# Order of X's updates, early squares, and two ordinary pairs ahead, in a Hymba-style encoder layer

## Chip, cores and metric

The kernel runs on one core of a Trainium2 chip (trn2). The metric is the device time of one execution in microseconds, the median of several runs. Beside the runs there is one profiled execution, whose span (first to last instruction) and trace are used for reading.

## Reference

One encoder layer over 256 tokens with a width of 2048, everything in fp32:

```python
for layer in range(DEPTH):          # DEPTH = 1
    ff = swiglu(rms_norm(x, pre_norm_ffn1), w_ffn1_gate_up, w_ffn1_down)     # D_FF = 5632
    x = x + 0.5 * rms_norm(ff, post_norm_ffn1)
    h = rms_norm(x, pre_norm_mix)
    q_h, i_h, f_fwd, f_bwd, g_h, q_a, k_a, v_a = split(h @ w_mix_in)
    y_h = hgrn2_mixer(...)          # gated linear recurrence, both directions, chunks of 64
    y_a = window_attention(...)     # 8 heads, 2 kv heads, +-128 tokens, sink and T5 bias
    x = x + rms_norm(concat(y_h, y_a) @ w_mix_out, post_norm_mix)
    ff = swiglu(rms_norm(x, pre_norm_ffn2), w_ffn2_gate_up, w_ffn2_down)
    x = x + 0.5 * rms_norm(ff, post_norm_ffn2)
return x
```

with `swiglu(x, wg, wd) = (silu(gate) * up) @ wd`. Nearly all of the work is in five large matrix products: two gate/up projections, two down projections and the mixer's two projections.

## The kernel before

**Products.** A fp32 product is made of three passes: each operand is split into a high part h (rounded to fp32r, a cast on ScalarE, L176) and the rest l (a subtraction on VectorE, L177), and TensorE adds h·h, h·l and l·h (`three`, L423; L352 to L354 for the mixer's first products, L299 and L304 elsewhere). The activations lie transposed in X^T as h and l parts (`xt` for X, `ht` for the FFN's inner values). Weights come in blocks of 1 MB: SP issues a DMA into `raw` (three buffers), ScalarE and VectorE split it into `h` and `l` (five buffers each).

**Pairs.** A down projection runs over 22 pairs, each two blocks of 128 of the 5632 inner columns, twice: run 0 for the first 1024 output columns, run 1 for the others. An ordinary pair costs 24 matmuls of 512 columns. A *seven* pair (the even ones below 20) saves three with a scheme of seven products in place of eight; for it VectorE makes in-place sums of the raw block (L455, L459, L461) and ScalarE and VectorE split those, and its first left operand with its right block is the separate `ha`, `la`. While a seven is split, the code already loads the ordinary pair that follows it and splits its first half (`begin_next`, `AHEAD`). The order of pairs is a list, `orders[0]` for run 0 and `orders[1]` for run 1, used by both FFNs. Pair 1 is worked first, then the transposes of the last gate/up group (silu at L884, L885, transposes at L896) and then `first_run` does the rest.

**End of a projection.** `Pairs.finish` ends run 1. It holds back the last two pairs and multiplies them block by block: m is a half of the 256 rows, n a half of the run's columns, q = 0..3 a quarter of X's 2048 columns. For each block it makes the row's sum of squares (`squares`, L612, ScalarE), multiplies by the gain (`gains`, L619, VectorE), and after both n it adds the normed result to X (`update(m, q)`, L666, VectorE). X's quarters are then transposed on TensorE (`turned(m, q)`, L210), and the new X^T is taken as h by ScalarE (`hi`, L227) and as l by VectorE (`lo`, L232). So that TensorE has work in between, the first products of the next projection are laid among these steps (`lead`, a `LeadN` for the mixer and a `Gated` for FFN2; `lead.more(i)` splits half of its second block, `lead.pieces(m, xt)` gives groups of products). This happens twice, behind FFN1 (707 to 741 us, "end 1") and behind the mixer (1125 to 1160 us, "end 2"). The end of FFN2 has code of its own.

In these blocks the order on TensorE, VectorE and ScalarE is the one written (`manual_schedule`), and instructions that come from outside of the block are filled in by the scheduler. Everywhere else the scheduler puts the instructions in order by its own costs. SP's loads go in the order of the program.

**Statistics of the next norm.** `pre_stats` (L240) makes the squares of X, eight of 512 columns on ScalarE (L249), then VectorE's sum, GpSimd's power and a copy into `rs2`. `spread` (L262) makes a diagonal matrix of them (`dg`, L267, VectorE), multiplies it by ones on TensorE (L268) to get the scales along the free axis, and copies these to `R`; X^T is multiplied by them later (`even`). It is done at the start, behind end 1 and behind end 2.

**Start.** X is loaded in pieces, transposed and taken while the first gate/up products run, in a block written by hand (L958 to L1020).

Of the kernel before, what the change touches and what calls it, by code (L numbers as in the profile page):

```python
# [11 lines left out]
F32 = mybir.dt.float32  # L12
# [3 lines left out]
BF16 = mybir.dt.bfloat16  # L16
AF = mybir.ActivationFunctionType
# [3 lines left out]
P = 128  # L21
D = 2048
# [3 lines left out]
EPS = 1e-6  # L26
# [11 lines left out]
def hymba_layer_kernel(  # L38
# [25 lines left out]
    nc = tc.nc  # L64
# [11 lines left out]
    def nm(s):  # L76
        uid[0] += 1
        return f"{s}_{uid[0]}"
# [11 lines left out]
    res = {"X": new_X()}  # L90
# [89 lines left out]
    def rsqrt_of(ssq, scale, eps):  # L180
        tot = stat.tile([P, 1], F32, tag="tot", name=nm("tot"))
        nc.vector.tensor_reduce(tot, ssq, axis=AX.X, op=ALU.add)
        v = stat.tile([P, 1], F32, tag="v", name=nm("v"))
        nc.vector.tensor_scalar(v, tot, scale, eps, ALU.mult, ALU.add)
        r = stat.tile([P, 1], F32, tag="r", name=nm("r"))
        nc.gpsimd.tensor_tensor(r, v, mhalf[:, 0:1], ALU.pow)
        return r
# [41 lines left out]
    def take_lo(*a):  # L229

        for src, g, hi, lo in take_views(*a):
            nc.vector.scalar_tensor_tensor(  # L232
                lo, src, g, hi.bitcast(F32), ALU.mult, ALU.subtract
            )
# [5 lines left out]
    def pre_stats():  # L240
        with tc.issue_after(last["act"].ins):
            pre_stats_now()

    def pre_stats_now():
        for m in range(2):
            ssq = stat.tile([P, 4], F32, tag="ssq", name=nm("ssq"))
            for q in range(4):
                jk = stat.tile([P, 512], BF16, tag="jk", name=nm("jk"), bufs=1)
                nc.scalar.activation(  # L249
                    jk, res["X"][:, m, q * 512 : (q + 1) * 512], AF.Square, accum_out=ssq[:, q : q + 1]  # L250
                )
            r = rsqrt_of(ssq, 1.0 / D, EPS)
            last["rs2"] = nc.vector.tensor_copy(rs2[:, m : m + 1], r)

    def power_and_rest():
# [284 lines left out]
    class Pairs(Blocks):  # L540
# [75 lines left out]
        def gains(self, m, n, dst=None):  # L616
            if dst is None:
                dst = self.y[m, 2 * self.now + n]
            nc.vector.tensor_tensor(  # L619
                dst, self.c[m][n], self.pg[:, n * 512 : (n + 1) * 512], ALU.mult  # L620
            )
# [9 lines left out]
        def finish(self, mul, post, new_x=None, gain=None, lead=None):  # L631


            order = self.orders[1]
            n_order = len(order)
            self.post = post
            self.work(n_order - self.HELD)
            held = []
            for u in order[n_order - self.HELD :]:
                held.append((u, *split_load(self.source(u), hp=post, lp=post)))  # L640
            close_far()
            self.half_gain(post)
            if new_x:
                new_x()
            X = res["X"]
            if lead:
                lead.load()
            r = [None, None]
            y = self.y

            def products(m, n, part):
                for u, k, hs, ls in [
                    (u, k, hs, ls) for u, hs, ls in held for k in range(2)
                ][part]:
                    self.plain(u, hs, ls, m, n, k)

            def squares(m, n):
                self.squares(m, n)
                if n == 1:
                    r[m] = rsqrt_of(self.ssq[m], 1.0 / (D * mul * mul), EPS / (mul * mul))  # L660

            gains = self.gains

            def update(m, q):
                sl = slice(q * 512, (q + 1) * 512)
                nc.vector.scalar_tensor_tensor(  # L666
                    X[:, m, sl], y[m, q], r[m], X[:, m, sl], ALU.mult, ALU.add
                )

            def update_aside(m, q):  # L670
                sl = slice(q * 512, (q + 1) * 512)
                nc.scalar.mul(y[m, q], y[m, q], r[m])
                nc.gpsimd.tensor_tensor(X[:, m, sl], X[:, m, sl], y[m, q], ALU.add)

            ordered = {mybir.EngineType.PE, mybir.EngineType.DVE, mybir.EngineType.Activation}
            every = slice(None)
            if gain is None:
                def store(m, q):
                    sl = slice(q * 512, (q + 1) * 512)
                    nc.sync.dma_start(out[0, m * P : (m + 1) * P, sl], X[:, m, sl])  # L680

                def in_place(n):
                    gains(1, n, dst=self.c[1][n])
                    y[1, 2 + n] = self.c[1][n]

                with tc.manual_schedule(engines=ordered):
                    products(0, 0, every)
                    squares(0, 0)
                    gains(0, 0)
                    products(0, 1, every)  # L690
                    squares(0, 1)
                    gains(0, 1)
# [24 lines left out]
            def hi(m, q):  # L717
                take_hi(m, q, gain, xt, banks[m, q])

            def lo(m, q):  # L720
                take_lo(m, q, gain, xt, banks[m, q])

            with tc.manual_schedule(engines=ordered):
                products(0, 0, every)
                squares(0, 0)
                gains(0, 0)
                products(0, 1, every)
                squares(0, 1)
                update(0, 0)
                gains(0, 1)  # L730
                products(1, 0, every)
                lead.more(0)
                update(0, 1)
                squares(1, 0)
                gains(1, 0)
                products(1, 1, slice(0, 3))

                def took(m, q):
                    hi(m, q)
                    lo(m, q)  # L740

                turned(0, 0)
                took(0, 0)
                products(1, 1, slice(3, None))
                turned(0, 1)
                squares(1, 1)
                took(0, 1)
                update(1, 0)
                update(1, 1)
                lead.more(1)  # L750
                first, second = lead.pieces(0, xt), lead.pieces(1, xt)
                next(first)
                next(first)
                turned(1, 0)
                took(1, 0)
                gains(1, 1)
                next(first)
                turned(1, 1)
                took(1, 1)
                for _ in first:  # L760
                    pass
                for m, q in ((0, 2), (1, 2), (0, 3), (1, 3)):
                    update(m, q)
                    next(second)
                    turned(m, q)
                    took(m, q)
                for _ in second:
                    pass
            return xt

# [66 lines left out]
    def ffn(gated, w_dn, post_gain, again, gain=None, lead=None, aside=None):  # L837

        with ExitStack() as st:
# [74 lines left out]
            for g in range(NG):  # L914
# [39 lines left out]
    xt = new_xt()  # L954
    gated.see(xt)
    with tc.manual_schedule():
        banks = {}

        def turned(*at):
            banks[at] = turn(*at)  # L960
# [48 lines left out]
        gated.piece(0, 1, 0)  # L1009
        gated.piece(0, 1, 1)  # L1010
        gated.parts[1] = split(raws[0])
        turned(0, 1)
        turned(1, 1)
        taken(0, 1)
        taken(1, 1)
        for k in range(2):
            for m in range(2):
                gated.piece(1, k, m)
        gated.parts[2] = split(raws[1])
        for k in range(2):  # L1020
            for m in range(2):
                gated.piece(2, k, m)
                turned(m, 2 + k)
# [503 lines left out]
```

## Time and profile before

| | |
|---|---|
| time, median of 3 runs | 1854.42 us (1854.17 to 1855.5) |
| profiled execution | 1853.69 us, span 1851.4 us |
| granted TensorE clock | 0.998 |
| TensorE / VectorE / ScalarE busy | 99% / 84% / 58% of the span |
| DMA | 365.78 MB, mean 198 GB/s |

A row of the timeline has the start in us from the span's start, the duration, engine, line, operation and the tiles out<-in; `x4` means four in a row; brackets give the engine's idle time just before it and what ended it. Matmuls overlap one another in the records, so their spacing is read from start to start. A row of the list of waits has the engine, its tile and line, what it waited for, and then the total us, how often, and the longest.

### The profile page before, as it was taken

The page shows a single profiled execution, that of the slowest core. Times are in us where ns is not written, and L with a number is a line of the kernel's source. Part 1 is how long each engine was busy: PE and PEld are TensorE (multiplying, and loading weights), DVE is VectorE, ACT ScalarE, POOL GpSimd, SP SyncE. Part 2 cuts the span into 40 slices and gives each one's busy share as a digit, 9 for nine tenths or more (in the row PEclk, how much of TensorE's full clock was granted, in tenths as well). Part 3 has the DMA queues.
Part 4 walks back from the last instruction along what each step waited for, and adds up shares of the span by engine and source line. Part 5 has one row for each costly group of instructions (what it writes and reads, how often), then busy time and mean ns, then how long its engine had stood idle before and what let it go on. Part 6 is the DMA issues. An engine that isn't in the chain of part 4 may idle for free.

```text
span 1851.4 us, 23247 instructions
## 1 busy us (share of the span) xinstructions
PE 1836.2 (99%) x8670; PEld 1533.2 (83%) x8670; DVE 1559.9 (84%) x1956; ACT 1079.3 (58%) x1429; POOL 20.6 (1%) x39
## 2 busy tenths in 40 slices
PE   9999999999999999999999999999999999999998
PEld 7888888888888887888888887888888888888886
DVE  7988888888899998577787788888888788899997
ACT  6555555555565655577677655655555555566563
POOL 1000000000000000000000000000000000000000
PEclk9999999999999999999999999999999999999999
DMA  7555555555565565555565555565555555555564
GB/s 253 205 197 189 205 204 182 182 190 200 190 227 212 198 255 197 194 177 166 169 186 157 172 208 200 182 214 186 210 206 194 204 184 206 190 183 207 217 249 156
DMA packets 180881, 365.78 MB, mean 198 GB/s; under 512 B 9257, under 2 KB 56449, under 8 KB 180001
## 3 DMA queue, kind: packets, MB, share of 16 engines
q1 hardware_dynamic: 180416, 364.17, 56.5%
q8 instruction: 68, 1.11, 0.2%
q14 instruction: 45, 0.36, 0.1%
q0 software_dynamic: 352, 0.14, 0.0%
HBM read 360.06 MB, written 4.21 MB: 197 GB/s over the span
## 4 chain that ended last, share of the span: by engine, by line
PE 95%; DVE 2%; ACT 1%; DMA 1%; issue 1%; POOL 0%; SPq 0%; DVEq 0%; ACTq 0%; POOLq 0%
PE pa L423 40%; PE pb L423 37%; PE pa L299 8%; PE pa L304 4%; PE pa L354 1%; PE pa L352 1%; PE pa L353 1%; DVE l L177 1%; PE pa L896 0%; PE pb L896 0%; ACT xt L227 0%; PE pb L1270 0%; PE pb L1248 0%; PE pb L1396 0%; ACT jk L249 0%
## 5 line engine op out<-in xcount | busy, mean ns | idle before, releaser
L176 ACT CAST h<-raw 128x1024 fp32r<-128x1024 f32 (+1 forms) x789 | 796.3, 1029 | 626.9 <-PE pb L423 344.4
L177 DVE TENSOR_TENSOR l<-raw,h 128x1024 fp32r<-128x1024 f32 (+1 forms) x789 | 923.3, 1193 | 202.7 <-ACT h L176 169.2
L423 PE MATMUL pa<-h,xt 128*128 128x512 f32 x1248 | 431.5, 392 | 0.0
L423 PE MATMUL pb<-h,xt 128*128 128x512 f32 x1168 | 407.2, 390 | 0.0
L423 PEld LDWEIGHTS pa<-h,xt 128*128 128x128 f32 x1248 | 234.4, 188 | 48.8 <-ACT h L176 0.8
L423 PEld LDWEIGHTS pb<-h,xt 128*128 128x128 f32 x1168 | 219.2, 188 | 45.5
L423 PE MATMUL pa<-l,xt 128*128 128x512 f32 x624 | 243.2, 390 | 0.0
L423 PE MATMUL pb<-l,xt 128*128 128x512 f32 x584 | 227.3, 389 | 0.0
L299 PE MATMUL pa<-xt,h 128*128 128x512 f32 x672 | 164.7, 394 | 0.0
L423 PE MATMUL pa<-h,ht 128*128 128x512 f32 x464 | 162.7, 389 | 0.0
L423 PE MATMUL pb<-h,ht 128*128 128x512 f32 x464 | 162.6, 389 | 0.0
L299 PEld LDWEIGHTS pa<-xt,h 128*128 128x128 f32 x672 | 123.0, 188 | 23.6
L423 PEld LDWEIGHTS pa<-l,xt 128*128 128x128 f32 x624 | 117.4, 188 | 23.8 <-DVE l L177 0.5
L423 PEld LDWEIGHTS pb<-l,xt 128*128 128x128 f32 x584 | 109.7, 188 | 22.6
L455 DVE TENSOR_TENSOR raw<-raw 128x1024 f32<-128x1024 f32 x84 | 102.8, 1223 | 2.2
L423 PEld LDWEIGHTS pa<-h,ht 128*128 128x128 f32 x464 | 87.1, 188 | 18.2
L423 PEld LDWEIGHTS pb<-h,ht 128*128 128x128 f32 x464 | 87.1, 188 | 18.0
L304 PE MATMUL pa<-xt,l 128*128 128x256 f32 x672 | 91.5, 285 | 0.0
L423 PE MATMUL pa<-l,ht 128*128 128x512 f32 x232 | 90.3, 389 | 0.0
L423 PE MATMUL pb<-l,ht 128*128 128x512 f32 x232 | 90.3, 389 | 0.0
L304 PEld LDWEIGHTS pa<-xt,l 128*128 128x128 f32 x672 | 87.1, 191 | 3.2
L423 PE MATMUL pb<-h,sp 128*128 128x512 f32 x176 | 61.8, 390 | 0.0
(280 smaller groups left out, 2133.0 us busy)
## 6 DMA issues: line engine op xcount, KB each, us to landing
raw<-in_w_ffn_gate_up_dram SPq DMA_DIRECT2D x350, 512.0 KB, 4.7
raw<-in_w_ffn_down_dram SPq DMA_DIRECT2D x88, 1024.0 KB, 5.0
raw<-in_w_mix_in_dram SPq DMA_DIRECT2D x52, 1024.0 KB, 4.9
raw<-in_w_mix_out_dram SPq DMA_DIRECT2D x16, 1024.0 KB, 5.0
pg<-in_post_norm_ffn_dram SPq DMA_DIRECT2D x4, 512.0 KB, 5.8
X<-in_x_dram SPq DMA_DIRECT2D x2, 1024.0 KB, 7.3
bias<-row SPq DMA_DIRECT2D x16, 128.0 KB, 4.6
kept<-X SPq DMA_DIRECT2D x2, 1024.0 KB, 4.8
```

Of the source, the lines that this page charges most:

```text
L176: nc.scalar.copy(hi, src)
L177: nc.vector.tensor_tensor(lo, src, hi.bitcast(F32), ALU.subtract)
L299: nc.tensor.matmul(slot[f], weights(hs, kk, f), xcol(xt, k), start=(k == 0), stop=(k == KT - 1))
L304: nc.tensor.matmul(slot[f][:, 0:T], weights(ls, kk, f), xcol(xt, kh * 8 + kk, 0), start=False, stop=False,)
L352: nc.tensor.matmul(dst, xh, h[:, o : o + n], start=(k == 0), stop=False)
L353: nc.tensor.matmul(dst, xh, l[:, o : o + n], start=False, stop=False)
L354: nc.tensor.matmul(dst, xl, h[:, o : o + n], start=False, stop=(k == KT - 1))
L423: nc.tensor.matmul(self.bank(at), lhs, rhs, start=(n == 1), stop=n in (ends, self.of[at]), skip_group_check=n > ends,)
L455: nc.vector.tensor_tensor(four[:, 0:2], four[:, 0::3], four[:, 1:2].to_broadcast([P, 2, 512]), ALU.add)
```

## The change

- **Ends.** In `finish`, `lead.more(0)` and `lead.more(1)` come before `update(0, 0)`. `update(0, 2)` and `update(0, 3)` directly follow `update(1, 1)`; `update(1, 2)` and `update(1, 3)` follow `lo(1, 1)`. `lo(0, 0)` and `lo(0, 1)` are cut into halves, and `update(1, 0)` is put between halves. `turned(1, 0)` comes behind three groups of lead products instead of two; the remaining pieces of the first row half come last.
- **Squares.** The eight squares of X can be made one by one (`square_x(m, q)`), and `pre_stats_now` makes only those that are left. Four of them are put into the ends and two into the start.
- **First down run.** `orders[0]` begins with pairs 1 and 3, so that two ordinary pairs are worked before the first seven. From there on a seven and an ordinary pair alternate, with pairs 8 and 10 next to each other; from 13 on the order is the old one.

```diff
+    squared = {}
+
+    def square_x(m, q):
+        if m not in squared:
+            squared[m] = (stat.tile([P, 4], F32, tag="ssq", name=nm("ssq")), set())
+        ssq, done = squared[m]
+        if q not in done:
+            done.add(q)
+            jk = stat.tile([P, 512], BF16, tag="jk", name=nm("jk"), bufs=1)
+            nc.scalar.activation(
+                jk, res["X"][:, m, q * 512 : (q + 1) * 512], AF.Square, accum_out=ssq[:, q : q + 1]
+            )
     def pre_stats_now():
         for m in range(2):
...
+                square_x(m, q)
+            r = rsqrt_of(squared.pop(m)[0], 1.0 / D, EPS)
...
                 products(0, 0, every)
                 squares(0, 0)
                 gains(0, 0)
+                lead.more(0)
                 products(0, 1, every)
                 squares(0, 1)
+                lead.more(1)
                 update(0, 0)
                 gains(0, 1)
                 products(1, 0, every)
-                lead.more(0)
                 update(0, 1)
                 squares(1, 0)
                 gains(1, 0)
                 products(1, 1, slice(0, 3))
                 turned(0, 0)
-                took(0, 0)
+                hi(0, 0)
                 products(1, 1, slice(3, None))
+                lo(0, 0, (0, 1))
                 turned(0, 1)
                 squares(1, 1)
-                took(0, 1)
+                hi(0, 1)
+                square_x(0, 0)
+                square_x(0, 1)
+                lo(0, 0, (2, 3))
+                lo(0, 1, (0, 1))
                 update(1, 0)
+                lo(0, 1, (2, 3))
                 update(1, 1)
-                lead.more(1)
+                update(0, 2)
+                update(0, 3)
                 first, second = lead.pieces(0, xt), lead.pieces(1, xt)
-                next(first)
-                next(first)
+                for _ in range(3):
+                    next(first)
                 turned(1, 0)
-                took(1, 0)
-                gains(1, 1)
+                hi(1, 0)
                 next(first)
+                lo(1, 0)
                 turned(1, 1)
-                took(1, 1)
-                for _ in first:
-                    pass
+                hi(1, 1)
+                square_x(1, 0)
+                square_x(1, 1)
+                gains(1, 1)
+                lo(1, 1)
+                update(1, 2)
+                update(1, 3)
                 for m, q in ((0, 2), (1, 2), (0, 3), (1, 3)):
-                    update(m, q)
                     next(second)
                     turned(m, q)
-                    took(m, q)
-                for _ in second:
+                    hi(m, q)
+                    lo(m, q)
+                for _ in (*first, *second):
                     pass
...
-                [1, 0, 3, 2, 5, 4, 7, 6, 9, 8, 11, 10, 13, 12, 15, 14, 17, 16, 18, 19, 20, 21],
+                [1, 3, 0, 5, 2, 7, 4, 9, 6, 11, 8, 10, 13, 12, 15, 14, 17, 16, 18, 19, 20, 21],
...
         gated.parts[1] = split(raws[0])
+        square_x(0, 0)
...
         gated.parts[2] = split(raws[1])
+        square_x(1, 0)
```

More of the change, by code (lines that the diff above doesn't have):

```diff
@@ L242, in pre_stats @@
             pre_stats_now()
+    squared = {}
[9 more added lines that the diff above has]
+            )
     def pre_stats_now():
         for m in range(2):
-            ssq = stat.tile([P, 4], F32, tag="ssq", name=nm("ssq"))
             for q in range(4):
[L248 to L252, printed above, removed]
+                square_x(m, q)
+            r = rsqrt_of(squared.pop(m)[0], 1.0 / D, EPS)
             last["rs2"] = nc.vector.tensor_copy(rs2[:, m : m + 1], r)
@@ L718, in hi, with lo @@
                 take_hi(m, q, gain, xt, banks[m, q])
-            def lo(m, q):
-                take_lo(m, q, gain, xt, banks[m, q])
+            def lo(m, q, js=range(4)):
+                take_lo(m, q, gain, xt, banks[m, q], js)
             with tc.manual_schedule(engines=ordered):
@@ L736, in finish @@
                 products(1, 1, slice(0, 3))
-                def took(m, q):
+                turned(0, 0)
+                hi(0, 0)
+                products(1, 1, slice(3, None))
+                lo(0, 0, (0, 1))
+                turned(0, 1)
+                squares(1, 1)
+                hi(0, 1)
[3 more added lines that the diff above has]
+                lo(0, 1, (0, 1))
+                update(1, 0)
+                lo(0, 1, (2, 3))
+                update(1, 1)
+                update(0, 2)
+                update(0, 3)
+                first, second = lead.pieces(0, xt), lead.pieces(1, xt)
+                for _ in range(3):
+                    next(first)
+                turned(1, 0)
+                hi(1, 0)
+                next(first)
+                lo(1, 0)
+                turned(1, 1)
+                hi(1, 1)
[5 more added lines that the diff above has]
+                update(1, 3)
+                for m, q in ((0, 2), (1, 2), (0, 3), (1, 3)):
+                    next(second)
+                    turned(m, q)
                     hi(m, q)
                     lo(m, q)
-                turned(0, 0)
-                took(0, 0)
-                products(1, 1, slice(3, None))
-                turned(0, 1)
-                squares(1, 1)
-                took(0, 1)
-                update(1, 0)
-                update(1, 1)
-                lead.more(1)
-                first, second = lead.pieces(0, xt), lead.pieces(1, xt)
-                next(first)
-                next(first)
-                turned(1, 0)
-                took(1, 0)
-                gains(1, 1)
-                next(first)
-                turned(1, 1)
-                took(1, 1)
-                for _ in first:
-                    pass
-                for m, q in ((0, 2), (1, 2), (0, 3), (1, 3)):
-                    update(m, q)
-                    next(second)
-                    turned(m, q)
-                    took(m, q)
-                for _ in second:
+                for _ in (*first, *second):
                     pass
```

## The prediction

> **What bounds the kernel now.** I read the page first, then the chain of waits, then TensorE's waits, and then the timeline around each of them. The page's table of engines and its chain that ended last:
>
> ```profile
> PE 1836.2 (99%) x8670; PEld 1533.2 (83%) x8670; DVE 1559.9 (84%) x1956; ACT 1079.3 (58%) x1429; POOL 20.6 (1%) x39
> ...
> PE 95%; DVE 2%; ACT 1%; DMA 1%; issue 1%; POOL 0%; SPq 0%; DVEq 0%; ACTq 0%; POOLq 0%
> ```
>
> TensorE is busy for 1836.2 of 1851.4 us and is 95% of the chain. No engine beside it can gain or lose anything unless TensorE waits less or more. So the question is which of TensorE's waits the change takes away. From the list of TensorE's waits, the two entries that belong to the ends of the projections and to the spreading of the row scales (columns: total us, times, longest):
>
> ```profile
> PE pa L210 <- DVE X L666: 1.5, 2, 1.2
> PE pb L268 <- DVE dg L267: 1.4, 2, 0.8
> ```
>
> The second pair of such waits (pb, L210) and one at L423 stand in the same list. The timeline of TensorE gives each of them: start, duration, instruction, and in brackets the idle time and what ended it.
>
> ```profile
> 39.24 0.39 PE L423 MATMUL pa<-h,xt 128*128 128x512 f32 x1
> 40.32 0.38 PE L268 MATMUL pb<-dg,ones 128*128 128x128 f32 x1 [0.69 <-DVE dg L267]
> 718.98 0.39 PE L354 MATMUL pa<-h,xt 128*128 128x512 f32 x1
> 719.85 0.33 PE L210 MATMUL pb<-ident,X 128*128 128x128 f32 x1 [0.49 <-DVE X L666]
> 724.71 0.39 PE L354 MATMUL pa<-h,xt 128*128 128x512 f32 x1
> 725.38 0.33 PE L210 MATMUL pa<-ident,X 128*128 128x128 f32 x1 [0.28 <-DVE X L666]
> 731.92 0.39 PE L354 MATMUL pa<-h,xt 128*128 128x512 f32 x1
> 733.52 0.33 PE L210 MATMUL pa<-ident,X 128*128 128x128 f32 x1 [1.21 <-DVE X L666]
> 1138.28 0.33 PE L210 MATMUL pb<-ident,X 128*128 128x128 f32 x1 [0.49 <-DVE X L666]
> 1168.52 0.38 PE L268 MATMUL pb<-dg,ones 128*128 128x128 f32 x1 [0.76 <-DVE dg L267]
> 1634.69 0.61 PE L423 MATMUL pb<-h,sp 128*128 128x512 f32 x2
> 1635.99 0.50 PE L423 MATMUL pb<-l,sp 128*128 128x512 f32 x1 [0.68 <-DVE l L177]
> ```
>
> How long a matmul takes is read from the start of one pair's first product to the next one's; the seven products of pair 16 lie between the second and third of these rows (the first, for pair 8, is used further down):
>
> ```profile
> 1663.13 0.39 PE L423 MATMUL pa<-ha,ht 128*128 128x512 f32 x1
> 1703.93 0.39 PE L423 MATMUL pa<-ha,ht 128*128 128x512 f32 x1
> 1708.69 0.39 PE L423 MATMUL pa<-ha,ht 128*128 128x512 f32 x1
> ```
>
> 4.76 us for 21 matmuls is 0.2267 us each. T(m,q) stands for the four transposes (L210) of quarter q of X's row half m. Each stall, from start to start, is then: spread at the start 40.32 - 39.24 - 0.23 = 0.85; T(1,0) of end 1 0.64; T(0,2) 0.44; T(0,3) 1.37; T(1,0) of end 2, with the same bracket, 0.64; spread behind end 2, scaled from 0.85 by its bracket (0.76 for 0.69), 0.92; second seven pair of FFN2's first down run 1635.99 - 1634.69 - 2 x 0.227 = 0.85. **Together 5.7 us.** By the brackets alone it is 0.69+0.49+0.28+1.21+0.49+0.76+0.68 = 4.6 us. That is all that this change can reach; matmuls are neither added nor dropped. I take start to start, because it is what the next matmul sees, and keep 4.6 for the range.
>
> **Order in the ends (both of them).** The rows of VectorE that make T(1,0) and T(0,3) late in end 1:
>
> ```profile
> 714.90 0.69 DVE L619 TENSOR_TENSOR y<-pb,pg 128x512 f32<-128x512 f32 x1
> 716.40 1.12 DVE L232 SCALAR_TENSOR_TENSOR xt<-pa,cols,xt 128x128 fp32r<-128x128 f32 x4 [0.81 <-ACT xt L227]
> 729.21 1.21 DVE L177 TENSOR_TENSOR l<-raw,h 128x1024 fp32r<-128x1024 f32 x1
> 731.67 1.13 DVE L232 SCALAR_TENSOR_TENSOR xt<-pb,cols,xt 128x128 fp32r<-128x128 f32 x4 [1.25 <-ACT xt L227]
> 732.72 0.74 DVE L666 SCALAR_TENSOR_TENSOR X<-y,r,X 128x512 f32<-128x512 f32 x1
> ```
>
> Before, update(0,3) at 732.72 stands behind lo(1,2), which had to wait 1.25 us for ScalarE's hi(1,2), which waits for TensorE's transpose: a circle through three engines. In the changed order update(0,2) and update(0,3) follow update(1,1) at once, and the two of 0.74 us are done about 10 us before TensorE gets to T(0,3). Both stalls go: 0.44 + 1.37 = 1.81. T(1,0) gets a third group of lead products ahead of it, 6 x 0.2267 = 1.36 us, and update(1,0) passes half a set of lo (1.13/2 = 0.56): 1.92 against a stall of 0.64, so it goes with 1.3 to spare, in both ends: 1.28.
>
> What is late next: update(1,2) now stands behind lo(1,1). Walking VectorE's new order with these durations I get its end at 725.3 and T(1,2) at 726.0. That is 0.8 us of cover; it is the thinnest in the end.
>
> What it adds: lead.more(0) and more(1) go forward past update(0,0) and past the groups of squares, so two L177 of 1.21 us stand ahead of update(0,0). VectorE has room there (it idles for the squares), I see 0.9 us left at T(0,0), so nothing. The scheduler then puts another chunk's L177 behind gains(1,0), ahead of lo(0,0). The L619 of 714.90 lets the next instruction begin at about 715.4; 1.21 us more ends it at 716.54, where lo(0,0) began at 716.40: 0.14 late, and TensorE's second lead product waits for lo(0,0). Bounds: nothing, and 1.21 - 0.81 = 0.40 (the bracket at 716.40 is room). I take 0.14, which is the walk, twice: **-0.28**. The raw loads of these chunks leave SP some 9 us sooner, and the order of the others is kept; nothing is queued behind them that TensorE needs.
>
> **Squares of X.** One square and its read, from the groups of ScalarE between 30 and 41 us:
>
> ```profile
> L249 ACT ACTIVATE jk<-X 128x512 bf16<-128x512 f32 x8 | 5.0, 630 | 0.1
> L249 ACT ACTIVATION_READ_ACCUMULATOR jk<-X 128x1 f32 x8 | 1.5, 190 | 0.0
> ```
>
> That is 0.63 + 0.19 = 0.82. At the start two of eight go forward into these gaps:
>
> ```profile
> 14.88 1.14 ACT L227 ACTIVATE xt<-pa,gain 128x128 fp32r<-128x128 f32 x4 [0.93 <-PE pa L210]
> 19.59 1.05 ACT L176 CAST h<-raw 128x1024 fp32r<-128x1024 f32 x1 [0.31 <-DMA raw<-in_w_ffn_gate_up_dram]
> 37.84 0.19 ACT L249 ACTIVATION_READ_ACCUMULATOR jk<-X 128x1 f32 x1
> ```
>
> The first fits the 0.93 us ahead of hi(0,1) at 14.88. The second makes the cast of 19.59 late by at most 0.82 - 0.31 = 0.51; that cast had waited for a DMA, and the next ones do too, so the lateness is taken up. The last of the block ends at 37.84 + 0.19 = 38.03 now. Two squares fewer make that 36.4 and the cast that the new order lets follow instead of lead (1.05) 35.3. From the last square VectorE and GpSimd need until here:
>
> ```profile
> 39.58 0.15 DVE L253 COPY scales<-r 128x1 f32<-128x1 f32 x1 [0.67 <-POOL r L186]
> 39.98 0.48 DVE L267 TENSOR_SCALAR dg<-ident,scales 128x128 f32<-128x128 f32 x2
> ```
>
> 39.98 + 0.48 = 40.46, 2.4 us behind 38.03. So dg is ready between 37.7 and 38.8. The changed order asks for it three matmuls sooner, at 39.47 - 0.68 = 38.79. The stall of 0.85 goes; if an L177 still comes between, 0.5 of it stays. In end 2 the transposes themselves come 32 places sooner (the four of the last quarter no longer stand among products), so the last hi is done some 7 us sooner, and four of eight squares are done by then. TensorE asks for the spread about ten matmuls sooner (2.3 us). The stall of 0.92 goes with about 2 us in hand. Nobody else waits for these squares. In end 1 nothing waits for the spread.
>
> The chip's own rule that speaks against moved squares is a load of function tables; it is a rival below.
>
> **Two ordinary pairs first.** In FFN2 the stall comes from a late transfer, not from VectorE's load:
>
> ```profile
> 1632.49 2.95 ACT L176 CAST h<-raw 128x1024 fp32r<-128x1024 f32 x3 [4.62 <-DMA raw<-in_w_ffn_down_dram]
> ```
> ```profile
> 1633.57 3.50 DVE L177 TENSOR_TENSOR l<-raw,h 128x1024 fp32r<-128x1024 f32 x3 [0.93 <-ACT h L176]
> ```
>
> ScalarE waited 4.62 us for a raw that lands at 1632.4, VectorE 0.93 behind it. Raws have three buffers, and a seven pair holds its own through four in-place sums. With pair 3 in front, TensorE has 24 x 0.2267 = 5.44 us more work before the first seven, while VectorE pays two L177 (2.4). So the first seven begins 3.0 us better off, and the buffer of pair 1 and then that of pair 3 come free before any seven needs a load. A walk gives the last split of pair 2 at 1637.6 against its product at 1638.3. The 0.85 goes; the cover is 0.7. In FFN1 the same spot has no stall, so nothing is gained there. The second cast of pair 3 now stands ahead of the silu on ScalarE; its buffer comes free 12 matmuls before the silu's input, so silu isn't late. Later on sevens and ordinary pairs alternate as before, but 8 and 10 follow one another (a rival).
>
> **Sum.** 0.85 + 0.64 + 1.81 + 0.64 + 0.92 + 0.85 - 0.28 = 5.4 us. Against the profiled execution's own 1853.69 that is 1848.3; its median stands 0.73 higher, 1854.42, so **1849.0 us**. By brackets, 4.6 - 0.28 = 4.3: 1850.1.
>
> A sentence on a rule: the Trainium skill's page "TensorE: Matmul & The Clock Gate", section "Back-to-back issue gap", gives about 131 ns for a 512-column matmul in a sustained stream. By that, six more products would be 0.79 us of cover, and T(1,0) would go with 0.7 rather than 1.3 to spare. No run here shows such a rate: the row above has 227, and the trace decides.
>
> **Rivals.**
>
> *The wait moves on (0.20).* T(1,2) and T(1,3) take over what T(0,2) and T(0,3) lose, because update(1,2) and update(1,3) wait behind lo(1,1) as update(0,3) waited behind lo(1,2). For it: 0.8 us of cover is less than one L177 (1.21). Against: the chain through three engines is one step shorter. It gives back up to 1.81 in end 1, and with 0.5 left at the start 2.3: 1851.3.
>
> *Seven upon seven (0.09), slower.* In the new order pair 10 follows pair 8, in both FFNs, and a seven begins the next load early only when the next is ordinary. Lead is read from the last in-place sum (L461) to the pair's first product:
>
> ```profile
> 1661.55 0.68 DVE L461 TENSOR_TENSOR raw<-raw 128x512 f32<-128x512 f32 x1
> 1700.12 0.69 DVE L461 TENSOR_TENSOR raw<-raw 128x512 f32<-128x512 f32 x1
> 1707.42 0.69 DVE L461 TENSOR_TENSOR raw<-raw 128x512 f32<-128x512 f32 x1
> ```
>
> Pair 8: 1663.13 - 1661.55 = 1.58. Pair 16: 3.81. Pair 18, directly behind 16: 1.27, so two sevens in a row eat 2.54. If pair 10's raw must moreover be waited for, at
>
> ```profile
> raw<-in_w_ffn_down_dram SPq DMA_DIRECT2D x88, 1024.0 KB, 5.0
> ```
>
> 5.0 us, each run loses 2.54 + 5.0 - 1.58 = 6.0, two of them 11.9, less 5.4: 1860.9. It decides when pair 8's lead is under 2.54 and the raw is late. Against: pair 3 in front adds up to 3.0 of lead, three raw buffers let pair 10's load leave when pair 6 is done, and 16 and 18 pass now without a wait.
>
> *Nothing is gained (0.07).* FFN2's stall is a transfer's accident and returns elsewhere, and each end loses at lo(0,0) up to 0.40 and at update(0,0) what it wins: 1854.
>
> *Table loads (0.03).* A square between casts could need another function table. One load in the trace:
>
> ```profile
> 1186.70 1.28 ACT L884 ACT_TABLE_LOAD   x1
> ```
>
> At 1.28 us, twice at the start (with 1.64 of squares, less 1.24 of gaps) and at four blocks of squares in the two ends: 2.96 + 5.1 - 5.4 is 2.7 slower, 1857.1. Against it: eight squares alternate with casts in 30 to 41 us with 0.1 us of idle time ahead of them. The Trainium skill, "ScalarE: Activation LUTs", section "Table sets: the hidden batching unit", has the rule that a switch of sets costs a load, about 2.7 us, and that cheap functions are in every set; this trace shows less for the load, and none at a square.
>
> **Numbers.** Forecast 0.61, at 1848 to 1850.6. A measurement here can tell about 0.2%, 3.7 us, so faster means under 1850.7: the forecast and a quarter of the first rival, 0.65. Same: the rest of it, nothing gained, table loads, 0.26. Slower: 0.09. The low end takes away the 0.28 and allows for the 1.3 us by which the runs of before differ, 1847.5; the high end holds the first rival and reaches into the third, 1853.4, and leaves out about 2 in 10.
>
> **What would show it.** Right: the lists of TensorE's waits hold no L210 <- DVE X, no dg, and no l in the down run; the span falls to about 1846. Wrong: an X wait at T(1,2) or T(1,3); a dg wait at 39 us; a new wait at pair 10's first products, about 46 us behind the start of a down run's sevens; table loads at 14 or 19 us. Any of these above 2 us would break the forecast.

## Result and profile after

The changed kernel takes 1846.29 us (median of 6 runs, 1845.76 to 1847.52) where the kernel before takes 1854.26 (6 runs, 1854.06 to 1855.5): 8.0 us faster, ratio 0.9957 with a 95% interval of 0.9944 to 0.9970. The direction and the places were forecast, the size was not: 5.4 us were forecast, and 1846.29 lies below the range's low end of 1847.5. The profiled execution has a span of 1844.0 us instead of 1851.4, so its trace shows 7.4 of the 8.0; the execution of before that was profiled took 1853.69 us, 0.57 less than the median. The granted TensorE clock was 0.998 in both. Of the prediction's signs, the lists of waits came out as it said; the span, which it put at about 1846, went 2 us lower.

The page of the changed kernel, the rows of its engines and of its chain:

```profile
PE 1832.5 (99%) x8670; PEld 1532.8 (83%) x8670; DVE 1559.4 (85%) x1956; ACT 1078.7 (59%) x1429; POOL 21.4 (1%) x39
...
PE 96%; DVE 1%; ACT 1%; DMA 1%; SPq 0%; issue 0%; DVEq 0%; POOL 0%; ACTq 0%; POOLq 0%
```

The matmuls are the same 8670, TensorE's share is as high, and VectorE's and ScalarE's busy time is unchanged to 0.6 us. The whole list of TensorE's waits in the changed kernel:

```profile
PE pb L130 <- DVE idle L124: 1.4, 1, 1.4
PE pb L1415 <- ACT pt L1407: 0.4, 1, 0.4
PE pb L210 <- DMA X<-in_x_dram: 0.4, 1, 0.4
PE pa L210 <- DMA X<-in_x_dram: 0.2, 1, 0.2
```

No X of L676 (the former L666), no dg and no l are left. Three of the four belong to the first microseconds (start of the program and arrival of X), one to the mixer. TensorE's timeline at the places that the prediction names, in the changed kernel:

```profile
38.05 0.39 PE L433 MATMUL pb<-h,xt 128*128 128x512 f32 x1
38.28 0.38 PE L278 MATMUL pb<-dg,ones 128*128 128x128 f32 x2
...
714.77 0.40 PE L363 MATMUL pa<-l,xt 128*128 128x512 f32 x1
715.32 0.50 PE L364 MATMUL pa<-h,xt 128*128 128x512 f32 x1
...
718.85 0.39 PE L364 MATMUL pa<-h,xt 128*128 128x512 f32 x1
719.09 0.38 PE L210 MATMUL pb<-ident,X 128*128 128x128 f32 x2
...
724.34 0.40 PE L364 MATMUL pa<-h,xt 128*128 128x512 f32 x1
724.57 0.33 PE L210 MATMUL pb<-ident,X 128*128 128x128 f32 x1
...
726.21 0.39 PE L364 MATMUL pa<-h,xt 128*128 128x512 f32 x1
726.45 0.38 PE L210 MATMUL pa<-ident,X 128*128 128x128 f32 x2
...
1160.94 0.39 PE L433 MATMUL pb<-h,xt 128*128 128x512 f32 x1
1161.17 0.38 PE L278 MATMUL pb<-dg,ones 128*128 128x128 f32 x2
```

In order: the spread at the start follows its forerunner after 0.23 us (1.08 before); the second lead product of end 1 waits for lo(0,0), 0.32 beyond 0.23; T(1,0), T(1,2) and T(0,3) follow after 0.23 or 0.24; the spread behind end 2 after 0.23 (1.15 before).

### The profile page after: what moved, and what is told of

It is laid out like the page before. It is cut to its first block, busy times and chain, and to the rows that moved or that the text cites. A ratio compares the mean times of both kernels' runs of the same rounds, so it can differ in the third digit from the quotient of the medians.

```text
span 1844.0 us, 23256 instructions
## 1 busy us (share of the span) xinstructions
PE 1832.5 (99%) x8670; PEld 1532.8 (83%) x8670; DVE 1559.4 (85%) x1956; ACT 1078.7 (59%) x1429; POOL 21.4 (1%) x39
## 4 chain that ended last, share of the span: by engine, by line
PE 96%; DVE 1%; ACT 1%; DMA 1%; SPq 0%; issue 0%; DVEq 0%; POOL 0%; ACTq 0%; POOLq 0%
PE pa L433 41%; PE pb L433 38%; PE pa L309 7%; PE pa L314 4%; PE pa L364 1%; PE pa L362 1%; PE pa L363 1%; DMA bias<-row 1%; PE pa L913 1%; PE pb L913 1%; DVE l L177 0%; PE pb L1415 0%; PE pb L1289 0%; PE pb L1267 0%; ACT h L176 0%; PE pb L1351 0%
## 5 line engine op out<-in xcount | busy, mean ns | idle before, releaser
L433 PE MATMUL pa<-h,sp 128*128 128x512 f32 x176 | 61.3, 389 | 0.0
```

The source lines that it names most:

```text
L433: nc.tensor.matmul(self.bank(at), lhs, rhs, start=(n == 1), stop=n in (ends, self.of[at]), skip_group_check=n > ends,)
```

## Experiments

For all of them I also added up, stretch by stretch, how much later each matmul starts than an undisturbed one would after its forerunner (226.7 ns after one of 512 columns, 117 after 256, 109 after 128). It is called *excess* here, is worked out from the starts of all matmuls of a trace, and counts each delay with what trails behind it. The intervals of single parts are wide (some 3 us), so where a difference is small the excess of the traces decides, not the median of the runs.

**The three parts, one at a time.** The first down run's order alone:

```diff
-                [1, 0, 3, 2, 5, 4, 7, 6, 9, 8, 11, 10, 13, 12, ...
+                [1, 3, 0, 5, 2, 7, 4, 9, 6, 11, 8, 10, 13, 12, ...
```

> The kernel before with the new order of the first down run alone. Theory A (each wait that goes takes its restart with it, and small slow spots too that no list of waits names): the gain is what the traces of before and after differ by in the two first down runs, 1.28 in FFN2 and 0.24 in FFN1, together 1.5 us, 1852.7. Theory B (the prediction's terms are right part by part, and the surplus lies in places that the change does not touch, such as the arrival of X and of the first weights): 0.85, 1853.4. Rival C (seven upon seven): a new wait at pair 10, slower than 1854.3.

1852.37 us (11 runs, 1851.99 to 1853.0) against 1854.38 in the same job: 2.0 faster, ratio 0.9989 (0.9981 to 0.9998). The excess falls from 1.30 to 0.29 in FFN2's first down run and from 0.26 to 0.02 in FFN1's. The trace's 1.25 is close to A's 1.5 and more than B's 0.85; the runs' 2.0 is above both, but their interval, 0.4 to 3.5 us, holds both. C is out: there is no wait at pair 10.

The early squares at the start alone:

```diff
         gated.parts[1] = split(raws[0])
+        square_x(0, 0)
...
         gated.parts[2] = split(raws[1])
+        square_x(1, 0)
```

> The kernel before with the two early squares at the start alone. A: 0.94 between 30 and 60 us, 1853.3, and the first 30 us as in the kernel before within what runs differ by. B: 0.85, 1853.4. Rival D (the early squares also move something in the first 30 us, where the traces of before and after differ by 0.51): 1.45, 1852.8, with the 0.51 seen again in this trace. Table loads would show as rows at 14 and 19 us; none is expected.

1852.97 us (11 runs) against 1854.38: 1.4 faster, ratio 0.9991 (0.9982 to 1.0). Between 30 and 60 us the excess is 0.75 instead of 1.70; in the first 14 us it is 3.97 in this trace, between the 4.17 of before and the 3.66 of after, so D's 0.51 is not there as it was described; a second profile of the changed kernel (below) has 0.1 more there than the first of before. The 1.4 of the runs is nearer to D's number than to A's; the trace gives 0.95 of it, which is A's, and the interval, 0 to 3.3 us, does not tell them apart.

The ends alone are the new `finish`, with the old order of pairs and without any `square_x`.

> The kernel before with the new order of the ends, with no early square anywhere and the old order of pairs. A: end 1 gains 2.8 and end 2's transposes 0.9; if the earlier transposes are enough for the spread behind end 2 that gains 1.0 more: 1849.6, else 1850.6. B: 1.81 + 2 x 0.64 - 0.28 = 2.8, and 0.92 if the spread's wait goes too: 1850.5 or 1851.4. The waits of 39 us and of the FFN2 down run stay as they were.

1849.44 us (7 runs): 4.9 faster, ratio 0.9972 (0.9961 to 0.9983). A's better branch holds: excess 3.55 to 0.70 in end 1, 2.73 to 0.82 in end 2 with the spread behind it, and the spread there does not wait though no square was moved.

The changed kernel with the old order of pairs:

> The changed kernel with the old order of the first down run. A: 1.5 us slower than the changed kernel, 1847.8, with a wait for an l of L177 back in FFN2's first down run. B: 0.85 slower, 1847.1. C: not slower, or faster, as pairs 8 and 10 no longer follow one another.

1848.28 us (5 runs), 2.0 slower than the changed kernel's 1846.29. A's direction holds, the wait for an l is back (0.9), with 1.81 of excess in FFN2's first down run and 0.29 in FFN1's. The parts alone add up to 2.0 + 1.4 + 4.9 = 8.3, against 8.0 for all together: they hardly touch one another.

**Inside the ends.** Without the four early squares in the ends:

> The changed kernel without the four early squares in each end (the two at the start stay). Theory A: the spread behind end 2 no longer waits because the transposes come sooner; the squares are not needed. Time as the changed kernel, 1846.3, no dg wait. Rival (the squares are what removes it): a dg wait of up to 0.76 at the spread behind end 2, start to start 0.92 and 0.1 of restart, 1847.3.

1846.38 us (5 runs), as the changed kernel. When dg is ready, and when TensorE's spread begins, in this kernel:

```profile
1158.84 0.48 DVE L277 TENSOR_SCALAR dg<-ident,scales 128x128 f32<-128x128 f32 x2
```
```profile
1162.35 0.60 PE L278 MATMUL pb<-dg,ones 128*128 128x128 f32 x4
```

1159.32 against 1162.35: 3.0 us of room without the squares. They buy nothing in this program that the runs could tell.

The four updates back in the loop (`update(m, q)` ahead of `next(second)`, as before):

> The changed kernel with the four updates of the quarters 2 and 3 put back each before its own transposes. A: the waits at the transposes of the quarters 2 and 3 return in end 1, start to start 1.81 with 0.06 of restart each and the two small ones at an l (0.3 each, one per end): 2.5 slower, 1848.8. The prediction's terms alone: 1.81, 1848.1. Rival (the third group of lead products and the early more(1) have already broken the circle): under 0.5 slower.

1851.28 us (11 runs), 5.0 slower than the changed kernel, twice what A said. TensorE's timeline of this kernel at T(0,2) and T(0,3) of end 1:

```profile
723.10 0.40 PE L364 MATMUL pa<-h,xt 128*128 128x512 f32 x1
725.16 0.33 PE L210 MATMUL pa<-ident,X 128*128 128x128 f32 x1 [1.66 <-DVE X L676]
...
731.44 0.39 PE L364 MATMUL pa<-h,xt 128*128 128x512 f32 x1
732.81 0.44 PE L210 MATMUL pa<-ident,X 128*128 128x128 f32 x2 [0.99 <-DVE X L676]
```

From start to start beyond 0.23 these are 1.83 and 1.14, and lo(0,0) waits 0.89 there instead of 0.32; excess 4.44 in end 1, more than the 3.55 of before. In end 2 the excess is 1.3 higher than in the changed kernel, at three lead products, of which A had counted one (0.3). Part of end 1's may be chance: in this profile a cast waits 1.17 us for a load of the mixer's weights just ahead, which update(0,0) then follows late. The runs agree on the whole, though (1850.81 to 1852.12), so of the pieces taken out one by one the place of these updates is worth the most, and the rest of the new order relies on it.

T(1,0) behind two groups of lead products instead of three:

> The changed kernel with T(1,0) behind two groups of lead products, as before. A: the wait for update(1,0) comes back in both ends, 0.64 less the 0.56 by which update(1,0) passes half a set of lo, so 0.1 to 0.3 each with restart: 0.2 to 0.6 slower, 1846.5 to 1846.9. Rival (the passing of half a set does not count, as that half set waits for hi anyway): 0.70 each, 1.4 slower, 1847.7.

1846.52 us (5 runs, 1846.28 to 1846.82), and no X in the list of waits. The time lies in A's span, but its reason is not there: the excess of each end is only 0.07 above the changed kernel's. Then also update(1,0) back behind the whole of lo(0,1):

> The changed kernel with T(1,0) behind two groups of lead products and update(1,0) behind the whole of lo(0,1), both as before the change. Theory A: the wait for update(1,0) is back in both ends, 0.64 with 0.06 of restart each: 1847.7. Rival (it had gone for another reason, such as the L177 and the squares that no longer stand between): no X wait, 1846.4.

1847.54 us (5 runs), as theory A said; T(1,0) starts 0.51 late in both ends, and TensorE's list has the wait again:

```profile
PE pb L210 <- DVE X L676: 0.7, 2, 0.3
```

So with two groups it is the passing of half a set of lo that takes away the wait at T(1,0), and with that passing the third group of products is spare. Three groups without the passing were not run; 1.36 us of products against 0.51 suggests that they would do as well.

The wait at lo(0,0), first by letting gains(1,0) follow the first half of lo(0,0):

```diff
                 squares(1, 0)
-                gains(1, 0)
...
                 lo(0, 0, (0, 1))
+                gains(1, 0)
```

> The changed kernel with gains(1,0) behind the first half of lo(0,0), so that the L177 of the following chunk runs ahead of the time at which hi(0,0) is done. A: the wait of 0.32 at the second lead product and its 0.11 of restart go in both ends: 0.86 faster, 1845.4. Rival (update(1,0) becomes late, as its gain is made later): a wait at T(1,0) takes the place, no gain, 1846.3 or more.

1846.09 us (5 runs): the wait falls from 0.32 to 0.19, where it was before the change, not to nothing, so A holds for less than half of it; no wait at T(1,0) takes its place, so the rival fails. With T(0,0) three matmuls sooner on top (`slice(0, 2)`):

> The changed kernel with gains(1,0) behind the first half of lo(0,0), and T(0,0) one slice (three matmuls, 0.68 us) sooner. Theory A: what is left of the wait at the second lead product (0.19, once gains(1,0) is moved) is the chain from the transposes over hi to lo, and goes when that chain starts 0.68 sooner; with its 0.11 of restart it is 0.6 for the two ends against the gain move alone, 0.9 against the changed kernel: 1845.4. Rival (update(0,0) is then late for T(0,0), whose room was put at 0.9): a wait for X at T(0,0), no gain, 1846.1 or more.

1845.10 us (5 runs, 1844.78 to 1846.43) against 1853.98 in its job. The profile is of the slowest of the five, and by its excess the two ends together gain 0.2 on the changed kernel, so it does not show where the other 1 us of the median comes from. In it each theory is right in one end: in end 2 the excess falls from 0.82 to 0.42, in end 1 it rises from 0.72 to 0.89, with this wait in the list:

```profile
PE pa L210 <- DVE X L676: 0.3, 1, 0.3
```

T(0,0) starts 0.48 late there. The prediction put the room of update(0,0) at 0.9, and in the changed kernel that is right: it ends at 711.27 + 0.75 = 712.02, and T(0,0) starts here:

```profile
712.97 0.60 PE L210 MATMUL pa<-ident,X 128*128 128x128 f32 x4
```

That is 0.95, in both ends; with T(0,0) 0.68 sooner, 0.28 is left in end 2. In end 1 of this run update(0,0) is late because a cast on ScalarE, ahead of the squares that it needs, waited for a load:

```profile
707.96 1.05 ACT L176 CAST h<-raw 128x1024 fp32r<-128x1024 f32 x1 [1.30 <-DMA raw<-in_w_mix_in_dram]
```

In the changed kernel's profile that cast begins at 706.27 without a wait. The last variant takes the sooner T(0,0) in end 2 alone, side by side with the changed kernel:

> The changed kernel with gains(1,0) behind the first half of lo(0,0) in both ends, and T(0,0) three matmuls sooner in end 2 alone, where no X was late for it (in end 1 update(0,0) was, by 0.48). A: end 2 gains 0.40 as with T(0,0) sooner in both, end 1 gains 0.1 as with the gain alone: 0.5 faster than the changed kernel in the same job, 0.3 faster than with T(0,0) sooner in both. B: below what the runs differ by, not to be told from the changed kernel.

> The changed kernel again, in the same job as the one above, to compare the two directly, and for a second profile of it. A: 8.0 us faster than the kernel before, with none of the waits for X, dg and l that the change removes; the first 14 us and the mixer may differ by some tenths, as they do between all the profiles.

1845.78 us (5 runs, 1845.59 to 1846.46) against 1846.34 (5 runs, 1846.23 to 1846.69): 0.6 faster by the medians, though the ranges overlap, and as A said, with excess 0.65 and 0.41 in the two ends. A's further 0.3 against the variant before it is not seen; the two are the fastest, and between them the runs do not decide. The changed kernel itself is 8.0 faster again, and the waits that its second profile adds (an l, 0.5, and an xt, 0.2) lie in the first 14 us.

**What holds up FFN2's first down run.** Two kernels that leave out a load of the old order:

> The kernel before, where the raw block of pair 5 in the first down runs of both FFNs is filled with zeros by GpSimd instead of being loaded (the weights of pair 5 are left out of run 0). Theory A (the wait in FFN2's first down run comes from two loads that share the DMA engines, pair 2's and pair 5's, issued 1.1 us apart): pair 2's raw lands in about 4.9 us instead of 6.1 to 6.8, the wait falls from 1.3 to 1.9 us to 0.4 or less, 1853.0. Theory B (the load leaves too late, or the in-place sums of VectorE are behind, whatever the transfer takes): the wait stays, 1854.3.

1852.98 us (11 runs) against 1853.98, a difference that the interval (0.9985 to 1.0003) does not quite clear. The wait is gone (excess 0.25), but the reason named under A is not the one: pair 2's raw had long landed. What stood in the way was the first cast of pair 5, queued on ScalarE ahead of pair 2's last cast and waiting for pair 5's load. So the next run took away pair 4's load, which leaves 1.1 us behind pair 5's:

> The kernel before, where the raw block of pair 4 in the first down runs is filled with zeros by GpSimd instead of being loaded (the weights of pair 4 are left out of run 0). ScalarE's last cast of pair 2 stands behind the first cast of pair 5, whose load leaves when VectorE has done pair 0's sums; the loads of pairs 5 and 4 leave 1.1 us apart. Theory A (pair 5's load takes long because it shares the DMA engines with pair 4's): it lands in about 4.9 us instead of 6.1 to 6.8, and the wait in FFN2's first down run, 1.3 to 1.9 with its restart, falls to 0.3 or less; about 1853.0. Theory B (it leaves too late, whatever it takes): the wait stays at 1.0 or more, 1854.0.

1854.76 us (11 runs) against 1854.34, no gain. ScalarE's wait between 1620 and 1640 us, and TensorE's stall:

```profile
ACT h L176 <- DMA raw<-in_w_ffn_down_dram: 2.6, 1, 2.6
```
```profile
1638.07 0.50 PE L423 MATMUL pb<-l,sp 128*128 128x512 f32 x1 [0.67 <-DVE l L177]
```

Pair 5's load took 6.12 us from issue to landing without pair 4's load beside it, and 6.13 with it in the kernel before; sharing is out (A fails), and the stall stays as B said. But B's "whatever it takes" does not hold. FFN1 runs the same code, and pair 5's load leaves at the same place in both FFNs, 5.30 us after the first product of the first seven. ScalarE's row of FFN1 in the kernel before, to be set beside the 4.62 of FFN2:

```profile
504.92 2.96 ACT L176 CAST h<-raw 128x1024 fp32r<-128x1024 f32 x3 [3.42 <-DMA raw<-in_w_ffn_down_dram]
```

There the load took 4.93, and there is no stall. Seven traces have the old order with this load in it. In FFN1 it took 4.9 to 5.5 us, and the down run's excess was 0.26 to 0.63; in FFN2 it took 6.0 to 6.8, and the excess was 1.2 to 1.9. The excess follows the load: 0.63 at 5.51, 1.19 at 6.03, 1.30 at 6.13, 1.59 at 6.42, 1.81 at 6.55, 1.93 at 6.81. So the stall takes both: a load that leaves without room to spare, and a transfer that is about 1 us longer in FFN2. Why it is longer there is open; pair 4's load is not the reason, and neither is the pause in the queue ahead of it, 14.24 us in both FFNs.

The load leaves so late because it goes into the buffer of pair 0, which VectorE's sums and splits release at 1626.2 in the kernel before. In the new order it goes into the buffer of an ordinary pair, leaves at 1605.5, and ScalarE's casts around the second seven wait mostly for TensorE instead:

```profile
1625.75 1.05 ACT L176 CAST h<-raw 128x1024 fp32r<-128x1024 f32 x1 [0.18 <-DMA raw<-in_w_ffn_down_dram]
1628.04 1.06 ACT L176 CAST h<-raw 128x1024 fp32r<-128x1024 f32 x1 [1.23 <-PE pb L433]
```

**Is it the one execution?** The kernel before, profiled again twice:

> The kernel before, unchanged, profiled once more. Theory A (the waits that the prediction read from one execution differ between executions of the same code, and that one was on the low side): the spread at the start waits, with its restart, 0.95 to 1.85 and the second seven pair of FFN2 0.8 to 1.5. Theory B (they are the same each time, and the surplus of the parts comes from elsewhere): 0.95 and 1.1 again, within 0.1.

> As the run before it, a further execution: A, at least one of the two waits differs from the first profile by more than 0.3; B, both within 0.1.

From the list of TensorE's waits of the first of them:

```profile
PE pb L268 <- DVE dg L267: 1.7, 2, 0.9
PE pa L210 <- DVE X L666: 1.5, 2, 1.2
...
PE pb L210 <- DVE X L666: 1.0, 2, 0.5
PE pb L423 <- DVE l L177: 0.7, 1, 0.7
...
PE pa L423 <- DVE l L177: 0.3, 1, 0.3
```

The two have 1.91 and 1.90 us of excess between 30 and 60 us where the first profile had 1.70, and 1.27 and 1.19 in FFN2's down run where it had 1.30. So A fails as put, and so does B's 0.1 at the start: the unchanged code repeats its waits within about 0.2, and the first profile was on the low side at the start only. (FFN1's down run had 0.63 in one of them, from an l that the first profile doesn't have.) The larger values come in kernels in which something else was changed: 1.59, 1.93 and 1.81 in the old down run of FFN2, which go with the longer loads above, and 2.60 at the start with the new order of pairs, which stays unexplained.

## Why the prediction was right about the places and wrong about the size

| stretch | forecast | excess before, 3 profiles | after, 2 profiles | saved (means) |
|---|---|---|---|---|
| 30 to 60 us | 0.85 | 1.70, 1.91, 1.90 | 0.75, 0.75 | 1.1 |
| first down run, FFN1 | 0 | 0.26, 0.29, 0.63 | 0.02, 0.02 | 0.4 |
| end 1 | 2.3 | 3.55, 3.56, 3.56 | 0.72, 0.72 | 2.8 |
| end 2 and the spread | 1.4 | 2.73, 2.71, 2.73 | 0.82, 0.83 | 1.9 |
| first down run, FFN2 | 0.85 | 1.30, 1.27, 1.19 | 0.02, 0.02 | 1.2 |
| sum | 5.4 | | | 7.4 |

**The step that failed** is "Together 5.7 us. ... That is all that this change can reach." It added up the seven waits that the list names, each to the start of the instruction that had waited, and put everything else at nothing. The range's low end then added only the 0.28 and the 1.3 us by which runs differ, so it had no room for delays without an entry. The trace holds more in the same stretches. Three places of the kernel before, on TensorE's timeline:

```profile
727.50 0.39 PE L353 MATMUL pa<-l,xt 128*128 128x512 f32 x1
727.91 0.50 PE L354 MATMUL pa<-h,xt 128*128 128x512 f32 x1
728.25 0.39 PE L352 MATMUL pa<-h,xt 128*128 128x512 f32 x1
...
1624.23 0.82 PE L423 MATMUL pb<-h,sp 128*128 128x512 f32 x2
1624.89 0.40 PE L423 MATMUL pb<-h,ht 128*128 128x512 f32 x1
...
1636.33 0.40 PE L423 MATMUL pb<-h,sp 128*128 128x512 f32 x1
1636.57 0.40 PE L423 MATMUL pb<-h,ht 128*128 128x512 f32 x1
```

727.91 starts 0.19 late, below what the list of waits shows, and its follower another 0.11 late. In the first seven pair of the down run two products in a row take 0.66 from the first start to the next instruction instead of 0.45, 0.21 lost without a wait in any list; FFN1 has the same 0.20. Behind the stall of 1635.99, 1636.33 is 0.11 late. Summed: 0.06 behind each of four late transposes, 0.10 behind each of two spreads, 0.11 behind the l, 0.30 and 0.29 at two small waits in the ends, and 0.21 and 0.20 in the first sevens, together 1.5 us that go along with the listed waits. Of the rest of the 2.0 between 5.4 and 7.4, the start's higher mean and FFN1's further l are 0.1 each, and some 0.2 lies in delays too small to single out. The spans of the profiles differ by 1851.8 - 1844.2 = 7.6 in the means, and so do the times of just these executions; the medians of all runs differ by 8.0, and the profiles do not say where the last 0.3 to 0.4 lies. The parts' times exceed what their stretches save (against the means of before) by 0.7 for the order, 0.3 for the start and 0.2 for the ends, which is open too.

**Point by point.**

*Start.* Right. dg was said to be ready between 37.7 and 38.8 us, asked for at 38.79. VectorE's dg, at the start and behind end 2, in the changed kernel:

```profile
37.30 0.48 DVE L277 TENSOR_SCALAR dg<-ident,scales 128x128 f32<-128x128 f32 x2
...
1155.93 0.48 DVE L277 TENSOR_SCALAR dg<-ident,scales 128x128 f32<-128x128 f32 x2
```

37.30 + 0.48 = 37.78, against TensorE's 38.28. The first early square sits in its gap, with no table load around it:

```profile
13.79 0.62 ACT L254 ACTIVATE jk<-X 128x512 bf16<-128x512 f32 x1
14.31 0.19 ACT L254 ACTIVATION_READ_ACCUMULATOR jk<-X 128x1 f32 x1
14.41 1.12 ACT L227 ACTIVATE xt<-pa,gain 128x128 fp32r<-128x128 f32 x4
```

That answers the table-load rival, as does the count of table loads, 30 in each of the two kernels. The Trainium skill's page "ScalarE: Activation LUTs", section "Table sets: the hidden batching unit", says that cheap functions, of which it names relu, copy, identity and abs, are in every set. It does not name square; the rows here agree with its being one of them. A square between casts costs its own 0.8 here and nothing more.

*End 1 and 2.* Right that both circles break; the 0.14 charged at lo(0,0) was 0.13. T(1,0) had 1.3 to spare by forecast. The updates in the changed kernel's end 1, (0,0), (1,0), and (1,2) with (1,3):

```profile
711.27 0.75 DVE L676 SCALAR_TENSOR_TENSOR X<-y,r,X 128x512 f32<-128x512 f32 x1
...
716.92 0.74 DVE L676 SCALAR_TENSOR_TENSOR X<-y,r,X 128x512 f32<-128x512 f32 x1
...
723.77 1.41 DVE L676 SCALAR_TENSOR_TENSOR X<-y,r,X 128x512 f32<-128x512 f32 x2
```

update(1,0) ends at 717.66, T(1,0) starts at 719.09: 1.4. But update(1,2) ends at about 723.77 + 0.74 = 724.51 and T(1,2) starts at 724.57: 0.06, where 0.8 was forecast (its 725.3 and 726.0 give 0.7). That is no cover: the second transpose of T(1,2) is 0.055 late, the mark that a late first one leaves elsewhere. So the first rival ("the wait moves on") had a real reason and begins to act here, but costs 0.06 instead of up to 1.81. For the spread of end 2 the prediction credited sooner transposes and early squares together; the former are enough.

*Down run.* The 0.85 goes, as said, and "the stall comes from a late transfer" was right: it is pair 5's, 6.0 to 6.8 us long where FFN1's takes 4.9 to 5.5. "Not from VectorE's load" was half right, since the transfer can leave only when VectorE's sums give up its buffer.

*Seven upon seven.* Its arithmetic held and its condition didn't. Last in-place sums of pairs 8 and 10 in FFN2 and their first products, changed kernel:

```profile
1657.34 0.69 DVE L471 TENSOR_TENSOR raw<-raw 128x512 f32<-128x512 f32 x1
...
1664.65 0.69 DVE L471 TENSOR_TENSOR raw<-raw 128x512 f32<-128x512 f32 x1
```
```profile
1661.16 0.39 PE L433 MATMUL pa<-ha,ht 128*128 128x512 f32 x1
...
1665.92 0.39 PE L433 MATMUL pa<-ha,ht 128*128 128x512 f32 x1
```

Pair 8 has a lead of 3.82, pair 10 of 1.27: two sevens in a row eat 2.55 (2.54 forecast), and 3.82 is enough.

## What to carry to other kernels

A list of waits names only delays above a certain size: the 0.19 and 0.32 from start to start at lo(0,0) are in neither list, of before or of after. When TensorE bounds a kernel, add up how late every matmul starts in the stretch that a change touches, small delays and restarts included, and take that as the ceiling; here the first trace held 9.5 us of it in the five stretches, of which 7.2 went, where the list gave 5.7. When a cast waits for a load, ask which instruction stands behind it in the same queue, which buffer the load needed, and how long the same load takes elsewhere: the cure here was one ordinary block between, which lets the load leave earlier, while the transfer that made FFN2 stall and not FFN1 is still not understood. And check what a piece does alone: six moved squares looked like one idea, and four of them buy nothing.

## What was not expected of the hardware

After a wait the next product of 512 columns starts 0.11 us late as well, after a late transpose the second transpose 0.06 late. Loads of 1 MB of down weights mostly land 4.9 us after issue in the steady order of the changed kernel. One and the same load, pair 5's in the old order, took 4.9 to 5.5 us in FFN1 and 6.0 to 6.8 in FFN2, with the same pause ahead of it and also with no load beside it; the runs do not show why.
